# One late expert block of the first layer multiplied unsplit, in four f32 passes

## The chip, the cores and the metric

The kernel runs on one core of a Trainium2 chip. Times are device microseconds of that core. Before the change three runs gave a median of 1667.28 us (1667.20 to 1667.38). The profile is of one further execution of the same program.

## What is computed

The program is a two-layer transformer block over 256 latent tokens and 256 context tokens of width 1024, all in float32. Each layer mixes the tokens (layer 0 by a Fourier part and grouped-query attention, layer 1 by neighbourhood attention), normalises, and then sends every token through 8 of 64 small experts and through one shared expert. In layer 0 there are 512 tokens, so 4096 pairs of token and expert. The part that the change touches is the expert:

```python
def expert_block(args):
    tok, e = args
    xb = h_pad[tok]
    a = jax.nn.silu(xb @ w_gate[e]) * (xb @ w_up[e])   # 1024 -> 256, twice
    return a @ w_down[e]                                # 256 -> 1024
```

The results are weighted by the routing scores and summed per token, then layer 0 ends with a normalisation and layer 1 begins.

## The kernel before

**Jobs.** The experts of a layer are ranked by how many tokens they have, and packed by a fixed plan (class `Plan`) into jobs of 128 slots, in four lanes of 32. Layer 0 has 42 jobs (0 to 41). A job with two experts runs them beside one another in separate strips of TensorE; a job with one segment uses the full array (jobs 6, 11, 15, 20, 25, 29, 34 and 39 in layer 0). Job 39, the third from the end, is the last one with a single expert.

**The steps of a job j** stand in the loop in `moe` (L1780 and on). TensorE and SyncE follow the order in which the program is written there; VectorE, ScalarE and GpSimd are ordered by the planner. TensorE does: gate and up products of job j (16 products of 128x128 with 256 columns when it is a full-array job); the transposes of the token rows of job j+1 in two halves (`slots_T`, L1459); between them four pieces of the scatter of an earlier job and the transposes of the activations (`act_T`, L1308); the down products (4 of 512 columns); and then the rest of the earlier job's scatter (L1544). A scatter piece is two products with a selection matrix, whose sum VectorE adds to `acc` (L1536).

**Two ways to multiply.** A list `passes` holds 3 or 4 for each job. With 4 (`gate_up` L1337, `down` L1351) the float32 operands go to TensorE as they are, and the trace has two matmul records for each product. With 3 (`gate_up3`, `down3`) weights and activations are split into a high and a low float32r part: a cast on ScalarE and a subtraction on VectorE (`split`, L161), and then three products (`mm3`, L165 to L167), one record each. Gate and up take four splits of 128x1024, down takes two, `xT` (by `slots_T`) and `aT` (by `act_T`) are split as well. The parts of the weights live in the pool `k4` of 13 buffers and, for one of the six, in `t8` of four.

**Weights.** They come from memory on SyncE's queue, 1 MB at a time, into the ring `w8` of 11 buffers; `experts` issues those of a job, in the order gate, up, down, when buffers are free. A job with two experts takes six buffers, one with a single expert three. A buffer is free when its last reader is through: TensorE's products for 4 passes, the splits for 3. Behind the loads of job 41 stand, in the same queue, four reloads of the residual rows (`xr`, L1791) and the first weights of layer 1 (`preload_na`, L848 and L855).

**Other work beside the last jobs.** For some jobs the results were added to a table in memory instead (`send`). Those sums come back in four fetches of 1 MB (`fetch`, L1525) at jobs 35 to 38, and VectorE adds them one job later (`add_fetched`, L1533), so two additions of 128x1024 at each of jobs 36 to 39. After job 41 comes the normalisation of layer 0, a loop for overfull experts (`overflow_blocks`, L1642) at whose head all engines meet, and layer 1.

Of the kernel before, what the change touches and what calls it, by code (L numbers as in the profile page):

```python
# [118 lines left out]
def tile_block(ctx: ExitStack, tc: tile.TileContext, I, out):  # L119
# [940 lines left out]
    def moe(l, out_of, nt, mp, pre=lambda: None, post=lambda: None):  # L1060
# [156 lines left out]
        njob = len(jobs)  # L1217
# [457 lines left out]

        passes = []
        for sg_ in jobs:
            passes.append(3 if l == 0 and len(sg_) == 1 and len(passes) > 2 else 4)
        grp, sc = [], iter(())
        over = overflow()  # L1680
        LA = 3 if l == 0 else 2
# [253 lines left out]
    with tc.tile_pool(name="moe0", bufs=1) as mp:  # L1935
        normalize(moe(0, out0, 4, mp, preload_na, mods_na)[0], xt[:2])
# [3 lines left out]
    with tc.tile_pool(name="moe1", bufs=1) as mp:  # L1940
        y = moe(1, out1, 2, mp)[1]
        for t in range(2):
            for n in range(1 + t):
                r = slice(n * 512, n * 512 + D // (1 + t))
                S.dma_start(out[0, t * 128:t * 128 + 128, r], y[t][:, r])
# [85 lines left out]
```

## Time and profile before

| what | value |
| --- | --- |
| median of three runs | 1667.28 us |
| profiled execution | 1667.79 us |
| its span, first to last instruction | 1666.0 us |
| TensorE (PE) busy | 1560.8 us, 94% |
| VectorE (DVE) busy | 762.9 us, 46% |
| ScalarE (ACT) busy | 444.3 us, 27% |
| GpSimd (POOL) busy | 174.0 us, 10% |
| mean granted TensorE clock | 0.980 |
| memory traffic | 332 GB/s over the span |

Busy shares are means over stages that differ. TensorE is pipelined, so what counts for it is when one group starts after another, and where the trace shows it idle and what ended that. A timeline row gives the start in us, how long the group lasted, the engine, the line, what was written from what, how many instructions were merged into the row, and in brackets the idle time ahead of it with what ended it. PEld, the load of the stationary operand, runs beside PE. SPq is SyncE's queue of transfers. In a row of stretches, the number behind an engine is its busy time, PEclk is the granted TensorE clock as a share of full speed (1.00 is 2.4 GHz, 0.50 is 1.2 GHz), and DMA is the mean busy share of the 16 DMA engines.

### The profile page before, as it was taken

The page shows a single profiled execution, that of the slowest core. Times are in us where ns is not written, and L with a number is a line of the kernel's source. Part 1 is how long each engine was busy: PE and PEld are TensorE (multiplying, and loading weights), DVE is VectorE, ACT ScalarE, POOL GpSimd, SP SyncE. Part 2 cuts the span into 40 slices and gives each one's busy share as a digit, 9 for nine tenths or more (in the row PEclk, how much of TensorE's full clock was granted, in tenths as well). Part 3 has the DMA queues.
Part 4 walks back from the last instruction along what each step waited for, and adds up shares of the span by engine and source line. Part 5 has one row for each costly group of instructions (what it writes and reads, how often), then busy time and mean ns, then how long its engine had stood idle before and what let it go on. Part 6 is the DMA issues. An engine that isn't in the chain of part 4 may idle for free. (4 is left out here: it accounts for less than half of the span.)

```text
span 1666.0 us, 30733 instructions
## 1 busy us (share of the span) xinstructions
PE 1560.8 (94%) x12138; PEld 1005.9 (60%) x12138; DVE 762.9 (46%) x2077; ACT 444.3 (27%) x882; POOL 174.0 (10%) x162
## 2 busy tenths in 40 slices
PE   7999999999999999999998799999999988989995
PEld 5765687546556566565665577866756654546542
DVE  2475585425455445354566832347443422223225
ACT  2447311113132232232222243332222211112111
POOL 1003210123221121221110000011000000000000
PEclk9999999999999999999999899999999999999998
DMA  9947864799999999989998566247779999999994
GB/s 331 340 172 290 297 233 162 268 366 382 346 398 345 402 401 389 392 327 406 404 407 309 205 212 222 89 181 309 303 316 420 419 419 419 419 420 419 419 420 179
DMA packets 122819, 547.91 MB, mean 329 GB/s; under 512 B 12917, under 2 KB 21509, under 8 KB 74672
## 3 DMA queue, kind: packets, MB, share of 16 engines
q1 hardware_dynamic: 108032, 501.76, 75.6%
q0 software_dynamic: 14640, 44.15, 8.6%
q8 instruction: 97, 1.59, 0.4%
q14 instruction: 50, 0.41, 0.1%
HBM read 532.10 MB, written 21.58 MB: 332 GB/s over the span
## 5 line engine op out<-in xcount | busy, mean ns | idle before, releaser
L1337 PE MATMUL bank<-w,xT 128*32 128x256 f32 (+1 forms) x5696 | 462.8, 388 | 25.8 <-DMA w<-in_moe_w_up_dram 20.2
L1337 PEld LDWEIGHTS bank<-w,xT 128*32 128x32 f32 (+1 forms) x5696 | 276.5, 122 | 204.9 <-DMA w<-in_moe_w_up_dram 28.2
L1351 PE MATMUL bank<-w,aT 128*32 128x512 f32 (+2 forms) x1248 | 235.3, 599 | 3.0 <-ACT aT L1312 2.9
L1293 DVE SCALAR_TENSOR_TENSOR a<-s,wsl,bank 128x256 f32<-128x256 f32 x70 | 33.6, 480 | 407.4 <-ACT s L1292 407.4
L1292 ACT ACTIVATE s<-bank 128x256 f32<-128x256 f32 x70 | 26.9, 385 | 544.5 <-PE bank L1337 496.7
L1544 PE MATMUL bank<-yy,ss 128*128 128x512 f32 x560 | 159.0, 411 | 1.4 <-DVE yy L161 1.1
L1536 DVE TENSOR_TENSOR acc<-acc,bank 128x512 f32<-128x512 f32 x212 | 138.0, 683 | 43.3 <-PE bank L1544 41.6
L1351 PEld LDWEIGHTS bank<-w,aT 128*32 128x32 f32 (+2 forms) x1248 | 68.5, 123 | 120.0 <-issue 104.0
L1544 PEld LDWEIGHTS bank<-yy,ss 128*128 128x128 f32 x560 | 97.3, 191 | 25.9 <-DVE yy L161 5.0
L161 DVE TENSOR_TENSOR yy<-bank,yy 128x512 fp32r<-128x512 f32 x96 | 65.9, 689 | 91.7 <-ACT yy L161 91.7
L161 ACT CAST yy<-bank 128x512 fp32r<-128x512 f32 x96 | 56.2, 586 | 161.6 <-PE bank L1351 144.2
L1445 POOL DMA_INDIRECT xg<-h2d,idx x42 | 52.1, 1239 | 356.8 <-PE bank L1459 181.7
L161 DVE TENSOR_TENSOR wl<-half,wh 128x1024 fp32r<-128x1024 f32 x35 | 42.7, 1224 | 74.4 <-ACT wh L161 74.4
L1250 DVE TENSOR_SCALAR oh<-ib,pos 128x64 bf16<-128x64 bf16 (+3 forms) x432 | 68.7, 245 | 9.7 <-PE bank L1276 9.7
L1516 POOL DMA_INDIRECT accd<-yd,idx x37 | 59.4, 1605 | 128.0 <-issue 92.7
L165 PE MATMUL bank<-wh,hT 128*128 128x512 f32 x160 | 65.2, 407 | 1.7 <-ACT wh L161 1.1
L167 PE MATMUL bank<-wl,hT 128*128 128x512 f32 x160 | 63.4, 396 | 0.5 <-DVE wl L161 0.5
L166 PE MATMUL bank<-wh,hT 128*128 128x512 f32 x160 | 63.2, 395 | 0.3 <-DVE hT L161 0.2
L1485 PE MATMUL bank<-ohr,h2p 128*128 128x256 f32 x448 | 60.8, 289 | 0.0
L1485 PEld LDWEIGHTS bank<-ohr,h2p 128*128 128x128 f32 x448 | 55.3, 191 | 8.2 <-PE bank L1337 4.4
L1437 POOL TENSOR_TENSOR xr<-xr,tmp 128x512 f32<-128x512 f32 x2 | 3.3, 1649 | 478.2 <-DVE tmp L1436 478.2
L1459 PE MATMUL bank<-head,xg 128*128 128x128 f32 x336 | 52.1, 278 | 0.0
(362 smaller groups left out, 2313.2 us busy)
## 6 DMA issues: line engine op xcount, KB each, us to landing
w<-in_moe_w_gate_dram SPq DMA_DIRECT2D x128, 1024.0 KB
w<-in_moe_w_up_dram SPq DMA_DIRECT2D x128, 1024.0 KB
w<-in_moe_w_down_dram SPq DMA_DIRECT2D x104, 1024.0 KB
w<-in_w_mod_dram SPq DMA_DIRECT2D x24, 1024.0 KB
half<-in_na_w_in_dram SPq DMA_DIRECT2D x12, 1024.0 KB
mh<-in_w_mod_dram SPq DMA_DIRECT2D x12, 1024.0 KB
w<-in_w_mod_dram SPq DMA_DIRECT2D x16, 512.0 KB
row<-rowsd POOLq DMA_DIRECT2D x15, 512.0 KB, 8.3
```

The lines of the kernel that those rows point to most:

```text
L161: return A.copy(o_h, src), eng.tensor_sub(o_l, src, o_h.bitcast(F32))
L165: T.matmul(p, xh, wh, start=first, stop=False)
L166: T.matmul(p, xl, wh, start=False, stop=False)
L167: T.matmul(p, xh, wl, start=False, stop=last)
L1250: V.tensor_scalar(oh[:, 32 * lane:32 * (lane + m)], ib[:, off:off + 32 * m], pos[:, t, c:c + 1], None, op0=OP.is_equal)
L1337: T.matmul(p[sl, q * FF:q * FF + FF], xT(j, sl), ws[k][0][q][:, j], start=j == 0, stop=j == NJ - 1, **kw)
L1351: T.matmul(p[sl], aT[:, j, sl], d[:, n * 512:n * 512 + 512], start=j == 0, stop=j == 1, **kw)
L1445: G.indirect_dma_start(out=x, out_offset=None, in_=h2d[:n2, :], in_offset=bass.IndirectOffsetOnAxis(ap=idx_col, axis=0), bounds_check=n2 - ...
L1485: T.matmul(o, h2p[t][k][:, 2 * q + j], oh[:, t].rearrange("p a b -> p (a b)")[:, :n], start=t == 0 and k == 0, stop=t == nt - 1 and k == 1)
L1516: G.indirect_dma_start(out=accd[turn_[0]][:, :], out_offset=bass.IndirectOffsetOnAxis(ap=i_, axis=0), in_=y[32 * lane:32 * (lane + m)], in ...
L1536: add = {0: lambda t, r, p: V.tensor_add(acc[t][:, r], acc[t][:, r], p)}
L1544: T.matmul(p, ss[:, t * 128:t * 128 + 128], yy[:, q, r], start=k == 0 and q == 0, stop=k == len(grp) - 1 and q == 1)
```

## The change

The list `passes` gets 4 instead of 3 for a job with one segment when it is among the last three of the plan. In layer 0 this concerns job 39 alone; the other seven full-array jobs from 6 to 34 stay as they were, and layer 1 has 4 everywhere already. Job 39 then goes through `gate_up`, `down`, and the unsplit forms of `slots_T` (called at job 38) and `act_T`. The calls on SyncE's queue keep their order.

```diff
         passes = []
         for sg_ in jobs:
-            passes.append(3 if l == 0 and len(sg_) == 1 and len(passes) > 2 else 4)
+            passes.append(3 if l == 0 and len(sg_) == 1 and 2 < len(passes) < njob - 3 else 4)
```

The functions that job 39 leaves:

```python
def gate_up3(x, w):
    p = bank()
    for k in range(4):
        wh, wl = gu_parts(w, k)          # cast on ScalarE, subtraction on VectorE
        ...
        for j in range(4):
            ...
            mm3(o, x[0](J, ...), x[1](J, ...), wh[:, j], wl[:, j], J == 0, J == NJ - 1)
    return p

def down3(aT, w):
    ps = [bank(), bank()]
    for j in range(2):
        wh, wl = w_parts([128, D], w[1][:, j, :], V)
        for n in range(2):
            ...
            mm3(ps[n], aT[0][:, j, :], aT[1][:, j, :], wh[:, r], wl[:, r], j == 0, j == 1)
    return ps
```

## Rows read from the trace of the kernel before

**Rows 1.** First line of the page: span and instructions.
```profile
span 1666.0 us, 30733 instructions
```
**Rows 2.** Timeline of PE, job 38: gate and up, transposes, down, rest of the scatter.
```profile
847.23 7.13 PE L1337 MATMUL bank<-w,xT 128*64 128x256 f32 x64
854.28 0.66 PE L1459 MATMUL bank<-head,xg 128*128 128x128 f32 x4
...
857.39 3.65 PE L1351 MATMUL bank<-w,aT 128*64 128x512 f32 x16
860.97 2.11 PE L1544 MATMUL bank<-yy,ss 128*128 128x512 f32 x8
```
**Rows 3.** Timeline of PE, job 39 and the start of job 40.
```profile
862.92 0.28 PE L165 MATMUL bank<-wh,xT 128*128 128x256 f32 x1
...
866.37 0.58 PE L167 MATMUL bank<-wl,xT 128*128 128x256 f32 x1 [3.06 <-DVE wl L161]
...
869.53 0.28 PE L166 MATMUL bank<-wh,xT 128*128 128x256 f32 x1
...
873.36 0.60 PE L1459 MATMUL bank<-head,xg 128*128 128x128 f32 x4
...
876.33 0.39 PE L165 MATMUL bank<-wh,aTh 128*128 128x512 f32 x1
878.31 0.49 PE L166 MATMUL bank<-wh,aTl 128*128 128x512 f32 x1 [1.60 <-DVE aTl L161]
880.64 0.80 PE L167 MATMUL bank<-wl,aTh 128*128 128x512 f32 x1 [1.83 <-DVE wl L161]
881.24 0.63 PE L165 MATMUL bank<-wh,aTh 128*128 128x512 f32 x1
...
885.08 2.71 PE L1544 MATMUL bank<-yy,ss 128*128 128x512 f32 x8
887.72 7.13 PE L1337 MATMUL bank<-w,xT 128*64 128x256 f32 x64
```
**Rows 4.** Timeline of DVE at job 39: additions, then splits of the gate weights.
```profile
862.71 2.47 DVE L1536 TENSOR_TENSOR acc<-acc,bank 128x512 f32<-128x512 f32 x4
865.09 2.36 DVE L161 TENSOR_TENSOR wl<-w,wh 128x1024 fp32r<-128x1024 f32 x2
```
**Rows 5.** Busy times in stretches: after the first stall, job 38, job 39.
```profile
866.40:869.40 3.00, 3.00 (x14) 3.00 (x15) 2.83 (x3) 0.00 (x0) 0.00 (x0) 0.50 1.02 419
...
847.20:862.90 15.70, 15.70 (x107) 9.68 (x107) 9.96 (x17) 5.25 (x9) 2.13 (x3) 1.00 1.02 421
862.90:887.70 24.80, 18.31 (x87) 15.31 (x85) 16.88 (x22) 6.43 (x10) 1.05 (x2) 0.79 0.87 344
```
**Rows 6.** Timeline of PE in layer 1: a full-array job in four passes.
```profile
1272.67 7.17 PE L1337 MATMUL bank<-w,xT 128*128 128x256 f32 x32
1279.50 2.26 PE L1485 MATMUL bank<-ohr,h2p 128*128 128x256 f32 x16
...
1283.68 3.59 PE L1351 MATMUL bank<-w,aT 128*128 128x512 f32 x8
1287.11 0.25 PE L1276 MATMUL bank<-wt,oh 128*128 128x15 bf16 x4
```
**Rows 7.** Timeline of SyncE's queue: up and down weights of job 41.
```profile
867.48 2.87 SPq L1069 DMA_DIRECT2D w<-in_moe_w_up_dram  x2
881.75 9.99 SPq L1074 DMA_DIRECT2D w<-in_moe_w_down_dram  x2
```
**Rows 8.** Busy times in stretches of 5 us: two with little traffic.
```profile
885.00:890.00 5.00, 5.00 (x31) 3.42 (x31) 3.42 (x6) 0.59 (x1) 0.00 (x0) 0.84 0.18 72
...
920.00:925.00 5.00, 4.12 (x15) 1.73 (x12) 3.05 (x5) 0.83 (x2) 0.00 (x0) 0.93 0.00 0
```
**Rows 9.** Timeline of POOL: the last fetch; then the landing of tile `ad`.
```profile
858.33 1.10 POOL L1525 DMA_DIRECT2D ad<-accd  x2 [0.48 <-issue]
...
DMA to landing us min/median/max: 14.8/14.8/14.8
```

## The prediction

> **What bounds the kernel now.** I read the page first, then TensorE's timeline around job 39, then VectorE's over the same time, then the transfers. The span is 1666.0 us [rows 1]; the profiled execution took 1667.79 us, so 1.79 us lie outside the span, and it stands 0.51 us above the median of 1667.28. TensorE is busy in 94% of it, so a change counts if it lets TensorE's queue reach a later point sooner and nothing else has to be waited for there.
>
> Job 38 shows how a job runs undisturbed: it starts at 847.23 and the next at 862.92 (first row of rows 3), 15.69 us, with TensorE busy throughout at a clock of 1.00 and VectorE busy for 9.96 us [rows 2, 3, 5]. Job 39 starts at 862.92 and job 40 at 887.72: 24.80 us, mean clock 0.79 [rows 3, 5]. The reader should see three bracketed waits in it, all for VectorE: 3.06 us for the first low part of the gate weights, 1.60 for the low part of the activations, 1.83 for a low part of the down weights, together 6.49 us [rows 3]. VectorE is not idle then. At 862.71 it still has four additions of 2.47 us in all, and only at 865.09 does it begin the subtractions that TensorE wants [rows 4]. So in this stage VectorE sets the pace, and TensorE's clock falls behind each wait: 0.50 from 866.4 to 869.4 [rows 5], and the 512-column products at 881.24 last 0.63 us [rows 3].
>
> **The change, part by part.** (1) Gate and up. In layer 1 a full-array job does them unsplit: its 32 records start at 1272.67 and the next group at 1279.50, so 6.83 us [rows 6]. Job 39 took from 862.92 to 873.36, 10.44 us [rows 3]. Saved: 3.61 us.
>
> (2) Down. The same job in layer 1 takes 1283.68 to 1287.11, 3.43 us [rows 6]. Job 39 took 876.33 to 885.08, 8.75 us [rows 3]. Saved: 5.32 us.
>
> (3) The rest of the scatter behind it: 2.64 us in job 39 (885.08 to 887.72), 1.95 us in job 38 (860.97 to 862.92), the same eight products [rows 2, 3]. The former start at the lower clock that the waits left. Saved: 0.69 us, if no wait is left in the job. The piece between gate and down is 2.97 us in job 39 (873.36 to 876.33) and 3.11 in job 38 (854.28 to 857.39). I take job 38's, so 0.14 is lost.
>
> Sum: 3.61 + 5.32 + 0.69 - 0.14 = 9.48 us. As a check, 15.69 of job 38 less 0.22 (gate and up 7.05, from 847.23 to 854.28, to 6.83) and 0.15 (down 3.58, from 857.39 to 860.97, to 3.43) is 15.32, and 24.80 - 15.32 = 9.48.
>
> In other words the products themselves get dearer: 48 records at 0.120 us (869.53 to 873.36, 32 of them) are 5.75 us against 6.83, and 12 at about 0.214 (half of the 0.427 us at which they follow one another from 881.24 to 885.08 at the low clock) are 2.56 against 3.43. That is 1.95 us lost. It is repaid by 6.49 us of waits and by the clock, which makes up the rest.
>
> Here a rule can be weighed. The trace has a split product at 0.120 us for 256 columns and pass, an unsplit one at 6.83 / 16 = 0.427 us, a ratio of 1.19 to the 0.359 of three parts [rows 3, 6]. The Trainium skill, "FP8 and Floating Point Precision", section "TensorE Precision Notes", says that true FP32 takes four passes through the array. Taken as a price of four passes to the split's three it would make 5.75 into 7.67 us and 2.56 into 3.41, and the sum 8.7 instead of 9.48; the row of layer 1 has the very operation, so I go by that.
>
> (4) ScalarE and VectorE lose the splits: six of 128x1024, at 2.36 / 2 = 1.2 us each on VectorE [rows 4], two of `xT` and one of `aT`. TensorE then waits for none of them. What remains on it are the two copies of `xT` and one of `aT` by ScalarE, which job 38 does as well while TensorE is busy for all of its 15.70 us [rows 5]. VectorE has some 10 us of work in a job of 15.3.
>
> (5) What is late next. The last fetch is issued at 858.33 in two parts, 0.55 us apart, and landing takes 14.8 us [rows 9]: 873.1 and 873.7. Before, VectorE reached these additions late. Now the activations of job 39 are through at about 862.92 + 6.83 + 0.7 = 870.5, and VectorE may stand for up to 2.6 us before the first addition. Behind it on VectorE are the scatter's additions, which free accumulator banks. TensorE needs such a bank only at the second half of the scatter, behind down, at about 876.3, when at least one has been freed. Bounds: 0 and 2.6 us; I take 0.2, near the lower end, since job 38 has the same two additions with TensorE busy throughout [rows 5].
>
> (6) Transfers. The order on SyncE's queue stays. The up weights of job 41 wait for job 39's gate and up buffers: 867.48 and some 2.5 us later before; now gate is read out at 862.92 + 3.4 = 866.3 and up at 869.8, no later. Its first down weight waited for the splits until 881.75 [rows 7]; now it is free at 876.3, its second when job 40 has used a gate, 878.2 + 3.5 = 881.7 instead of 891.4. The engines idle at 885 to 890 (0.18) shows that the queue had nothing left over by then [rows 8], so the weights of job 40 and the up weights of job 41 had landed by about 883. Job 40's, issued before those, are needed from 878.2, job 41's up from 897.6 + 3.5. Cost: 0; without this cover job 40 would wait for at most the 885 - 878 = 7 us until the traffic falls.
>
> (7) Behind it. At 920 to 925 no transfer runs at all [rows 8]: layer 1's first weights are there before layer 0's end wants them, and all of layer 1 is issued behind the meeting of the engines at the loop. So a shift of layer 0's end moves layer 1 as a whole, its stretch bound by transfers too. What can differ is where the clock falls: the down products of job 41 and the first products of layer 1 run partly at the lower clock. The nearest size is the 3.00 us at 0.50 behind job 39's first wait, which costs 1.5 us [rows 5]: one such more or less, -1.5 to +1.5; I take 0.
>
> Forecast: -9.48 + 0.2 = -9.28 us. Span 1666.0 - 9.3 = 1656.7, execution 1667.79 - 9.3 = 1658.5, and 0.51 lower for the median: **1658.0 us**.
>
> **The rivals.** A: VectorE is late anyway. Then the same 6.49 us of waits stay, in front of the scatter or of job 40, and the clock falls behind them as before; what is left is the dearer product, so 1667.28 + 1.95 = 1669.2 at worst, and 1667.28 - 9.48 + 6.49 = 1664.3 if the clock holds. For it: VectorE carries the fetched additions in these jobs. Against it: job 38 has them too, and 9.96 of 15.70 us [rows 5]. 5%.
>
> B: The gain is given back in front of layer 1, because its first weights or the residual rows come when they came before: 1667.3. For it: the DMA engines are at 1.02 through job 38 [rows 5]. Against it: they fall to 0.18 and later to 0.00 [rows 8], and what they wait for moves forward with the jobs. 4%.
>
> C, on the other side: the clock. Unsplit products at full array might be granted 1.2 GHz, as in the stretch at 0.50 [rows 5]. If the whole of job 39 ran so, it would take 2 x 15.32 = 30.6 us, 5.8 more than now: 1673.1. It turns slower when more than 9.5 of the 15.3 us are lost, so when over 62% of the job runs at the low clock. For it: this is where the clock falls now. Against it: each fall has a wait of TensorE ahead of it, job 38 in unsplit products stands at 1.00, and layer 1's full-array job runs at 0.2135 us a record, 512 columns at 2.4 GHz [rows 5, 6]. 4%. The Trainium skill, "TensorE: Matmul & The Clock Gate", Part 1, holds that idleness brings the throttle and activity releases it; by that rule C falls away, and the rows of job 38 and 39 agree.
>
> That the change touches nothing can be excluded: job 39 has one segment and stands at 42 - 3.
>
> **How the numbers follow.** The forecast has 87%. Its own bounds are the 2.6 us for the fetch in place of 0.2 and 1.5 us of clock either way: -9.48 - 1.5 = -11.0 gives 1656.3, -9.48 + 2.6 + 1.5 = -5.4 gives 1661.9. For the order that the planner gives VectorE and ScalarE, which this profile can't show, I add some tenths below. The range is 1655.5 to 1662.0; the rivals lie outside it with 13%. A measurement of this kernel can tell about 0.2%, 3.3 us, from no change. Faster by more than that: the forecast and a small part of A, 0.88. Within: most of A, and B, 0.08. Slower: C, 0.04.
>
> **What would show it.** Job 39 should start at about 863 and job 40 15.3 us later, with 32 records of gate and up over 6.8 us and 8 of down over 3.4, no wait for VectorE above 0.5 us between them, and a clock of 1.00. The zero traffic ahead of the loop and everything in layer 1 should come 9 to 9.5 us sooner. A wait of VectorE for the fetched sums of about 2.5 us may appear. The prediction is wrong if job 40 starts later than 881, if TensorE waits for a bank or a weight there, or if job 39 is short and layer 1 doesn't move with it.

## The result, and the profile after

The change took the median from 1667.28 us to 1657.09 (five runs, 1656.43 to 1660.99), a ratio of 0.994 with an interval of 0.9928 to 0.9952. The forecast was 1658.0. In a second measurement on another occasion it was 1657.65 against 1667.16, again 0.994 (0.9927 to 0.9954). The profiled execution took 1656.43 us, 1654.3 of them the span, 11.7 less than the span of before [rows 1].

TensorE's timeline of the changed kernel, job 39 from 862.50 and the start of job 40 (columns as in [rows 3]):

```profile
862.50 7.07 PE L1337 MATMUL bank<-w,xT 128*128 128x256 f32 x32
869.40 0.60 PE L1459 MATMUL bank<-head,xg 128*128 128x128 f32 x4
...
872.35 3.59 PE L1351 MATMUL bank<-w,aT 128*128 128x512 f32 x8
875.38 2.40 PE L1544 MATMUL bank<-yy,ss 128*128 128x512 f32 x8
877.71 7.13 PE L1337 MATMUL bank<-w,xT 128*64 128x256 f32 x64
```

No row has a bracketed wait, nor has any of the rows left out. The job takes 15.21 us (862.50 to 877.71) where it took 24.80 [rows 3]. VectorE in the same stretch:

```profile
870.48 1.22 DVE L1533 TENSOR_TENSOR acc<-acc,ad 128x1024 f32<-128x1024 f32 x1
871.61 0.68 DVE L1536 TENSOR_TENSOR acc<-acc,bank 128x512 f32<-128x512 f32 x1
873.29 1.23 DVE L1533 TENSOR_TENSOR acc<-acc,ad 128x1024 f32<-128x1024 f32 x1 [1.00 <-DMA ad<-accd]
```

It now stands for 1.00 us for the second fetched sum, and TensorE's rows above have no wait for it. Busy times in job 39, and at the place where layer 0 ends (PE, PEld, DVE, ACT, POOL, PEclk, DMA, GB/s):

```profile
862.50:877.70 15.20, 15.20 (x67) 11.44 (x65) 8.51 (x14) 3.10 (x6) 0.00 (x0) 1.00 1.02 414
...
910.00:915.00 5.00, 4.12 (x17) 2.73 (x16) 4.05 (x7) 0.59 (x1) 0.00 (x0) 1.00 0.00 0
```

The clock is at 1.00 throughout the job, against a mean of 0.79 [rows 5], and transfers run dry before layer 0 ends, as in [rows 8]. The timeline of SyncE's queue for the same loads as in [rows 7]:

```profile
866.14 3.79 SPq L1069 DMA_DIRECT2D w<-in_moe_w_up_dram  x2
875.98 5.77 SPq L1074 DMA_DIRECT2D w<-in_moe_w_down_dram  x2
```

The down weights go out 5.8 us sooner, at once when job 39's down products have read theirs. TensorE's timeline at the job of layer 1 that [rows 6] show:

```profile
1260.80 7.17 PE L1337 MATMUL bank<-w,xT 128*128 128x256 f32 x32
```

It started at 1272.67 and now starts at 1260.80, 11.87 us sooner, about as much as the whole span is shorter. So nothing was given back in layer 1. Job 39 itself accounts for 9.59 us of the 11.87. It began 0.42 sooner already, by chance (job 0 was 1.8 us sooner in this execution, ahead of everything that the change touches), and the down products of job 41 ran at the full clock this time, 3.65 us in the timeline of after:

```profile
906.60 3.65 PE L1351 MATMUL bank<-w,aT 128*64 128x512 f32 x16 [0.75 <-ACT aT L1312]
```

The same products in the timeline of before took 5.35 us:

```profile
916.59 5.35 PE L1351 MATMUL bank<-w,aT 128*64 128x512 f32 x16 [0.76 <-ACT aT L1312]
```

Together they are 11.7 us. The first experiment shows that the 1.7 us are not the change's.

### The profile page after: what moved, and what is told of

The parts are those of the page before. It is cut to its first block, busy times and chain, and to the rows that moved or that the text cites. A ratio compares the mean times of both kernels' runs of the same rounds, so it can differ in the third digit from the quotient of the medians.

```text
span 1654.3 us, 30681 instructions
## 1 busy us (share of the span) xinstructions
PE 1557.6 (94%) x12118; PEld 1002.7 (61%) x12118; DVE 754.4 (46%) x2068; ACT 438.1 (26%) x876; POOL 173.6 (10%) x162
## 5 line engine op out<-in xcount | busy, mean ns | idle before, releaser
L1337 PE MATMUL bank<-w,xT 128*32 128x256 f32 (+2 forms) x5728 | 473.0, 391 | 23.0 <-DMA w<-in_moe_w_up_dram 18.6
L1337 PEld LDWEIGHTS bank<-w,xT 128*32 128x32 f32 (+2 forms) x5728 | 285.3, 124 | 203.3 <-issue 30.3
L1292 ACT ACTIVATE s<-bank 128x256 f32<-128x256 f32 x70 | 26.9, 384 | 543.7 <-PE bank L1337 491.9
```

The costliest lines, as they stand in the source:

```text
L1337: T.matmul(p[sl, q * FF:q * FF + FF], xT(j, sl), ws[k][0][q][:, j], start=j == 0, stop=j == NJ - 1, **kw)
```

## The experiments

All ratios are against runs of the kernel before on the same chip; the medians of those lay between 1667.16 and 1668.83 us.

### The change again

No edit.

> The changed kernel once more, as the yardstick for the runs beside it. Theory (VectorE's lateness and the clock behind it were the price of the split): about 1657, and job 39 takes 15.2 us with the clock at 1.00. What differs between executions should be where the clock falls behind job 39: in the profile of the change the down products of job 41 took 3.65 us, in that of the kernel before 5.35; if this is chance and not the change, some executions of either kernel have it.

Measured: 1657.65 us, 0.994 (0.9927 to 0.9954). Job 39 from 865.24 to 880.46 is 15.22 us. TensorE's timeline at the start of jobs 39 and 40 and at job 41:

```profile
865.24 7.07 PE L1337 MATMUL bank<-w,xT 128*128 128x256 f32 x32
...
880.46 7.13 PE L1337 MATMUL bank<-w,xT 128*64 128x256 f32 x64
...
908.09 0.50 PE L1308 MATMUL bank<-head,a 128*128 128x128 f32 x2 [1.09 <-DVE a L1293]
909.35 5.33 PE L1351 MATMUL bank<-w,aT 128*64 128x512 f32 x16 [0.75 <-ACT aT L1312]
```

The same program has 5.33 us here and had 3.65 in the execution shown above, behind the same two waits of 1.09 and 0.75 us. The mean clock is 0.76 from 908 to 915 here and was 1.00 from 905.3 to 912.3 there. So where the clock falls behind job 39 differs from execution to execution. Of the twelve profiles in this document five have 5.3 us at this place (the one of before among them) and seven 3.65, all behind the same two waits. This execution also reached job 39 2.7 us later than the first. Its span is 1658.5 us, 4.2 more than the first. The runs of the changed kernel spread by about 5 us, so single executions can't be compared to better than that; the length of job 39 within them can.

### Each half alone

Gate and up unsplit, down split (the changed kernel with three passes in the down half of job 39):

```diff
+        pdown = [3 if l == 0 and j == njob - 3 else q for j, q in enumerate(passes)]
...
-                aT = act_T(a, passes[j])
+                aT = act_T(a, pdown[j])
...
-                ps = down3(aT, ws[0]) if passes[j] == 3 else down(aT, ws, segs)
+                ps = down3(aT, ws[0]) if pdown[j] == 3 else down(aT, ws, segs)
```

> Job 39 multiplies gate and up unsplit in four passes, down still split in three. Theory: about 3.5 us less than before from gate and up (10.44 to 6.9 us); VectorE, rid of four subtractions, is then in time for the down parts as well, so most of the 1.60 and 1.83 us of waits and the low clock go too: 1659 to 1661. Rival (each half pays for itself alone): 1667.3 - 3.6 = 1663.7, and the down half still takes 8.7 us.

Measured: 1664.62 us, 0.9987 (0.9975 to 0.9999), 0.9 us above the rival's number and 3.6 above the upper end of the theory's. TensorE's timeline, job 39 and the start of job 40:

```profile
861.30 7.07 PE L1337 MATMUL bank<-w,xT 128*128 128x256 f32 x32
868.21 0.60 PE L1459 MATMUL bank<-head,xg 128*128 128x128 f32 x4
...
874.43 0.50 PE L166 MATMUL bank<-wh,aTl 128*128 128x512 f32 x1 [2.87 <-DVE aTl L161]
876.76 0.80 PE L167 MATMUL bank<-wl,aTh 128*128 128x512 f32 x1 [1.82 <-DVE wl L161]
881.19 2.49 PE L1544 MATMUL bank<-yy,ss 128*128 128x512 f32 x8
883.62 7.13 PE L1337 MATMUL bank<-w,xT 128*64 128x256 f32 x64
```

Gate and up take 6.91 us as forecast, but the job is 22.32 us long, only 2.48 shorter than before. The first wait of down grew from 1.60 us [rows 3] to 2.87, so the down half takes 10.02 us (871.17 to 881.19) where the rival had it at 8.7. VectorE shows why:

```profile
869.28 1.22 DVE L1533 TENSOR_TENSOR acc<-acc,ad 128x1024 f32<-128x1024 f32 x1
870.41 0.68 DVE L1536 TENSOR_TENSOR acc<-acc,bank 128x512 f32<-128x512 f32 x1
872.22 1.23 DVE L1533 TENSOR_TENSOR acc<-acc,ad 128x1024 f32<-128x1024 f32 x1 [1.13 <-DMA ad<-accd]
873.36 0.68 DVE L1536 TENSOR_TENSOR acc<-acc,bank 128x512 f32<-128x512 f32 x1
873.96 0.42 DVE L161 TENSOR_TENSOR aTl<-bank,aTh 128x256 fp32r<-128x256 f32 x1
```

The low part of the activations stands behind two fetched additions, and the second of these waits for its transfer. TensorE came sooner and met a queue that could not come sooner. My theory for this run had taken VectorE's queue as work alone and left the transfer out.

Gate and up split, down unsplit (the kernel before, with the same three lines but `pdown = [4 if l == 0 and j == njob - 3 else q ...]`):

> Job 39 multiplies gate and up split in three passes, down unsplit in four. Theory: the wait of 3 us in gate stays, with the low clock behind it; down goes from 8.75 to 3.4 us and the scatter behind it to 1.95: 1667.3 - 6 = 1661.3, between 1660.5 and 1662.5. Rival (the waits move on to the scatter and to job 40 because VectorE stays late): 1664 or more.

Measured: 1661.13 us, 0.9966 (0.9953 to 0.9979): 6.0 us less than before, as the theory had it. TensorE's timeline:

```profile
862.31 0.28 PE L165 MATMUL bank<-wh,xT 128*128 128x256 f32 x1
...
865.71 0.58 PE L167 MATMUL bank<-wl,xT 128*128 128x256 f32 x1 [3.00 <-DVE wl L161]
...
875.72 3.60 PE L1351 MATMUL bank<-w,aT 128*128 128x512 f32 x8
878.75 2.40 PE L1544 MATMUL bank<-yy,ss 128*128 128x512 f32 x8
881.08 7.13 PE L1337 MATMUL bank<-w,xT 128*64 128x256 f32 x64
```

In these rows of TensorE's timeline the wait in gate is there, 3.00 us, and the down half has none. The two halves alone are worth 2.48 us and (862.31 to 881.08) 24.80 - 18.77 = 6.03; together 8.5, while the whole change shortens the job by 9.59. The rest, 1.1 us, is what the gate half loses again: 1.27 us in the down split's longer wait, less 0.21 that it gains in the scatter behind it (2.43 us for 2.64).

### Why VectorE was late

The kernel before, job 39 split, without the fetched additions of jobs 38 and 39. Two of the four token tiles lack the sums that were sent to memory.

```diff
+                if l == 0 and j in (njob - 4, njob - 3):
+                    added.clear()
                 add_fetched()
```

> The kernel before, three passes in job 39, but the sums that were fetched for two of the four token tiles are not added at jobs 38 and 39 (four additions of 1.22 us on VectorE are left out). Theory (VectorE is late at job 39 because of its queue, and the split alone is not dear): the first wait falls from 3.06 to about 0.6 us, those of down from 3.43 to under 1.8, the clock holds in part: 1658 to 1661, nearly the gain of the change with the split kept. Rival (the split of the job is too slow by itself, casts and parts come one by one): waits of over 5 us stay, 1665 or more.

Measured: 1658.97 us, 0.995 (0.9936 to 0.9965). TensorE's waits in job 39, with its first row and that of job 40:

```profile
863.34 0.28 PE L165 MATMUL bank<-wh,xT 128*128 128x256 f32 x1
...
866.42 0.39 PE L167 MATMUL bank<-wl,xT 128*128 128x256 f32 x1 [1.25 <-DVE wl L161]
...
874.51 0.50 PE L166 MATMUL bank<-wh,aTl 128*128 128x512 f32 x1 [0.54 <-DVE aTl L161]
876.84 0.50 PE L167 MATMUL bank<-wl,aTh 128*128 128x512 f32 x1 [0.44 <-DVE wl L161]
...
879.78 7.13 PE L1337 MATMUL bank<-w,xT 128*64 128x256 f32 x64
```

Four additions of 1.22 us, 4.9 us of VectorE, are gone, and with the split kept TensorE's job shrinks by 24.80 - 16.44 = 8.36 us (863.34 to 879.78). The waits fall from 6.49 to 2.23 us, 4.26 (the first is 1.25 us where 0.6 was expected). The other 4.1 are the clock: the same products keep TensorE busy for 14.27 us where it was 18.31 [rows 5], and the busy times of its job 39 show

```profile
863.30:879.80 16.50, 14.27 (x89) 11.86 (x88) 12.71 (x19) 5.52 (x9) 1.06 (x2) 1.00 1.01 415
```

a clock of 1.00, where it was 0.79 [rows 5]. It did not fall behind the wait of 1.25 us here; in job 39 of before it was low behind the wait of 3.06 us, and behind that of 1.83 with one of 1.60 shortly ahead of it [rows 3].

More changed than the length of VectorE's work. Without the additions the planner also sets VectorE's instructions in another order, and in VectorE's timeline the first subtraction for job 39's gate weights stands in job 38,

```profile
859.46 1.22 DVE L161 TENSOR_TENSOR wl<-w,wh 128x1024 fp32r<-128x1024 f32 x1
```

ahead of the scatter's last additions, where it was at 865.09 behind them [rows 4]. So the run shows that VectorE's queue made the split dear, and not how much of the 8.36 us is the additions' own and how much the new order's.

The changed kernel, job 39 unsplit, with the six weight splits still made for nobody:

```diff
+                if l == 0 and j == njob - 3:
+                    for k in range(4):
+                        gu_parts(ws[0], k)
                 p = pre_p.pop(j, None) or (gate_up3(xT, ws[0]) if passes[j] == 3 else gate_up(xT, ws, segs))
...
+                if l == 0 and j == njob - 3:
+                    for k in range(2):
+                        w_parts([128, D], ws[0][1][:, k, :], V)
                 ps = down3(aT, ws[0]) if passes[j] == 3 else down(aT, ws, segs)
```

> The changed kernel, job 39 unsplit, but the six weight splits (cast on ScalarE, subtraction on VectorE, 128x1024 each) are still made at job 39 and their parts are read by nothing. Theory (what cost was that TensorE waited for parts at the end of VectorE's queue, not the work itself): TensorE meets no part, only accumulator banks that VectorE frees later; job 39 takes 15.3 to 17.5 us and the whole 1657 to 1660. Rival (VectorE's and ScalarE's work itself holds the jobs up, through banks, through buffers of k4 or through the weight buffers that the splits keep): job 39 takes 20 us or more, 1662 to 1667.

Measured: 1658.18 us, 0.9952 (0.9939 to 0.9966). TensorE's timeline at the start of jobs 39 and 40, and the busy times of job 39:

```profile
863.78 7.07 PE L1337 MATMUL bank<-w,xT 128*128 128x256 f32 x32
...
879.00 7.13 PE L1337 MATMUL bank<-w,xT 128*64 128x256 f32 x64
...
863.80:879.00 15.20, 15.20 (x67) 11.44 (x65) 12.23 (x16) 5.44 (x9) 1.06 (x2) 1.00 1.01 415
```

VectorE does 12.23 us of work instead of the 8.51 of the changed kernel, and the job takes 15.22 us all the same (863.78 to 879.00). That is 3.7 us more and not the 7.2 of six splits, since the first ran in job 38 (from 861.01) and the last two, from 877.34 to 879.69, pushed other work into job 40. Job 40 takes 19.42 us, as in the changed kernel, so nothing is paid there either. The weight splits as work cost TensorE nothing; what cost was that it stood for their results. The splits of `xT` and `aT` are not in this run.

Gate and up unsplit, down split, and the fetches one job earlier:

```diff
-                if sent and j - max(sent) in range(2, 2 + nt):
-                    fetch(j - max(sent) - 2)
+                if sent and j - max(sent) in range(1, 1 + nt):
+                    fetch(j - max(sent) - 1)
```

> As in the run with gate and up unsplit and down split, and the four fetches of sums are issued one job earlier (jobs 34 to 37 instead of 35 to 38), so that VectorE has no such additions at job 39. Theory (in the run before, the wait for the activation's low part grew from 1.60 to 2.87 us because the second fetched addition stood 1.13 us for its transfer and two additions of 1.22 us lay ahead): the waits of down fall from 4.69 us to about 1.0, as in job 34, job 39 takes about 16 us, the whole 1657 to 1659. Rival (the down split is late whatever VectorE has ahead of it): waits above 3 us stay, 1663 or more.

Measured: 1658.25 us, 0.9954 (0.994 to 0.9967), 6.4 us less than the same kernel with the fetches where they were. TensorE's timeline at the start of job 39, at down, and at the start of job 40:

```profile
862.96 7.07 PE L1337 MATMUL bank<-w,xT 128*128 128x256 f32 x32
...
873.78 0.50 PE L166 MATMUL bank<-wh,aTl 128*128 128x512 f32 x1 [0.56 <-DVE aTl L161]
876.11 0.50 PE L167 MATMUL bank<-wl,aTh 128*128 128x512 f32 x1 [0.42 <-DVE wl L161]
...
879.07 7.13 PE L1337 MATMUL bank<-w,xT 128*64 128x256 f32 x64
```

The waits of down fall from 4.69 us to 0.98 and the job, 862.96 to 879.07, to 16.11. Nothing is left out here, so the finding of the run without the fetched additions doesn't hang on the missing sums. The edit takes the additions and the wait for their transfer out of job 39 together; what each of the two cost was not tried.

### The other full-array jobs

All eight unsplit (`passes.append(4)`):

> All eight full-array jobs of layer 0 multiply unsplit. By the rows, a job that is not disturbed takes about 5.8 + 4.5 us split (0.9 us of it waits for the parts of activation and down weights) and 6.83 + 3.43 us unsplit, the same; the seven jobs have 13 us of waits in all, of which some 4 are beyond that. Theory (the split is worth nothing where VectorE is busy, and nothing is lost by leaving it): 1653 to 1658, same as the change or a little less. Rival (three passes are the cheaper way where VectorE is in time, by 1.95 us a job): 1657 + 7 x 1.95 = 1671.

Measured: 1649.75 us, 0.9904 (0.989 to 0.9919), and in a second measurement, for which this stood,

> All eight full-array jobs of layer 0 unsplit, once more, beside the mixed version on the same chip: 1649 to 1651, and 8 us under the change by jobs 6 to 34.

1649.84 us, 0.9894 (0.9877 to 0.991). That is 7.3 us under the change's median, which was measured on another occasion, and below the 1653 to 1658 of the first expectation. In the profiles the time from the silu of job 5 to that of job 35 is 417.33 and 417.35 us with all unsplit, and 425.76 and 424.24 in the two of the changed kernel, so 6.9 to 8.4 us less. Down unsplit in all eight, gate and up split in the other seven:

```diff
+        pdown = [4] * njob
...
-                aT = act_T(a, passes[j])
+                aT = act_T(a, pdown[j])
...
-                ps = down3(aT, ws[0]) if passes[j] == 3 else down(aT, ws, segs)
+                ps = down3(aT, ws[0]) if pdown[j] == 3 else down(aT, ws, segs)
```

> The changed kernel, and the other seven full-array jobs keep gate and up split in three passes but multiply down unsplit in four. By the rows down is 4.5 us split, waits of 0.9 included, and 3.43 unsplit, so about 1.1 us a job. Theory (TensorE's queue sets the pace in layer 0): 7 x 1.1 = 7.7 us less than the change, about 1650. Rival (the transfers, at a busy share of 0.98 from 340 to 800 us, set it): about 1657, and waits for weights appear.

Measured: 1652.87 us, 0.9921 (0.9907 to 0.9934), 4.2 us under the change's median instead of 7.7. To see where, I took the time from one silu (ScalarE, L1292) to the next but one, which holds gate and up of the job and its down:

| job | 6 | 11 | 15 | 20 | 25 | 29 | 34 | 39 |
| --- | --- | --- | --- | --- | --- | --- | --- | --- |
| before | 27.78 | 27.30 | 31.16 | 27.10 | 27.08 | 29.66 | 26.91 | 40.43 |
| change | 27.78 | 28.84 | 29.66 | 27.10 | 27.09 | 31.13 | 26.91 | 30.91 |
| all unsplit | 26.98 | 26.27 | 27.95 | 27.45 | 27.23 | 27.24 | 27.24 | 30.91 |
| down unsplit, gate split | 27.00 | 26.53 | 28.86 | 26.29 | 27.41 | 30.26 | 26.10 | 30.92 |

Where a split job runs undisturbed, with no wait in gate and up (20, 25, 34), unsplit is 0.15 to 0.35 us dearer. Where it isn't (15 and 29) unsplit is 1.7 to 3.9 us cheaper. My expectation had taken jobs 6, 11, 15 and 29 for less disturbed than they are. In the timeline of the changed kernel TensorE begins job 29 like this:

```profile
714.57 0.39 PE L165 MATMUL bank<-wh,xT 128*128 128x256 f32 x1 [1.66 <-ACT wh L161]
715.83 0.39 PE L167 MATMUL bank<-wl,xT 128*128 128x256 f32 x1 [0.76 <-DVE wl L161]
```

and the run with only down unsplit keeps such waits, 30.26 us (and has one of 0.74 us at job 25). With all eight unsplit no wait for parts is left.

The first two lines of the table differ by up to 1.5 us at jobs 11, 15 and 29, where both kernels do the same. That is the clock again. In the kernel before, TensorE waits 1.66 and 0.76 us at job 29 just as above; the busy times around it, first before and then after, show

```profile
716.00:724.00 8.00, 6.81 (x54) 6.56 (x55) 4.87 (x6) 3.66 (x6) 0.00 (x0) 1.00 1.01 426
714.00:722.00 8.00, 6.67 (x41) 6.47 (x42) 4.93 (x5) 3.36 (x4) 0.00 (x0) 0.79 1.02 428
```

a clock of 1.00 in the one execution and 0.79 in the other. The two profiles of the kernel with all unsplit agree to 0.01 us at all eight jobs.

Split gate and up only where they paid, in jobs 20 and 34, everything else unsplit (the last kernel with `passes.append(3 if l == 0 and len(passes) in (20, 34) else 4)`):

> Each full-array job of layer 0 in the form that its own rows favour: down unsplit in all eight, gate and up unsplit in six, split at jobs 20 and 34 only, where the step took 26.29 and 26.10 us with the split gate against 27.45 and 27.24 without it. Theory (TensorE's queue sets the pace, so the steps' savings add up): 2.3 us under the run with all eight unsplit. Rival (what one job saves the next waits for, or the transfers at a busy share of 0.99 take it): the same as that run within 1 us.

Measured: 1645.88 us, 0.9872 (0.9855 to 0.9889), beside 1649.84 for all unsplit on the same chip. From the silu of job 5 to that of job 35 it takes 415.04 us against 417.33, 2.29 less, and the two steps are 26.27 and 26.10 us, so the savings added up as expected. Of the rest of the 4 us, 1.5 in the two profiles lie ahead of job 5, where both kernels do the same. This is the fastest version tried, 11 us under the change's median, which was measured on another occasion.

## Why the prediction was right

**Gate and up, down.** Forecast savings were 3.61 and 5.32 us. Gate and up now take 6.90 us (862.50 to 869.40) for 10.44, down 3.03 (872.35 to the next group at 875.38) for 8.75. By the records the scatter behind down starts 0.4 us earlier than I had it and lasts 2.33 us, to 877.71; the two together are 5.36 us, and the steps gave 5.38. The sum was 9.48, measured was 9.59, and three other profiles of unsplit jobs 39 agree (15.22, 15.22, and 30.91 over the two steps with all unsplit). The layer 1 job was the right row to price by, and with the count of passes in the Trainium skill ("FP8 and Floating Point Precision", "TensorE Precision Notes") as a price the sum of 8.7 would have been 0.9 too low.

**The split's own price.** I put the products at 1.95 us dearer unsplit, which treats the split form as free of waits. In the traces of before and after every split job has waits for its parts. Even in job 34 of the changed kernel, with VectorE in time, TensorE's timeline has waits in down:

```profile
796.02 0.50 PE L166 MATMUL bank<-wh,aTl 128*128 128x512 f32 x1 [0.56 <-DVE aTl L161]
796.36 0.40 PE L167 MATMUL bank<-wl,aTh 128*128 128x512 f32 x1
...
797.52 0.40 PE L166 MATMUL bank<-wh,aTl 128*128 128x512 f32 x1
798.35 0.50 PE L167 MATMUL bank<-wl,aTh 128*128 128x512 f32 x1 [0.43 <-DVE wl L161]
```

The table shows an undisturbed split job only 0.15 to 0.35 us cheaper. The split products of down were mis-sized as well. I had halved the 0.427 us of the low clock to 0.214; at the full clock the six from 796.36 to 797.52 follow one another at 0.232, so twelve are 2.8 us and not 2.56, and the 1.95 should have been 1.7. That step mis-sized the alternative, not the forecast, which took both lengths from rows.

**VectorE late, and the clock behind it.** The runs show this: leaving out 4.9 us of additions with the split kept, in an order that the planner changed with it, gave 8.36 us; splits that nobody waits for cost nothing; and fetching one job earlier took 3.7 us of waits out of the split down half. The prediction's words that the clock falls behind each wait go too far. In job 39 of before it did so at two of the three: behind that of 1.60 us it was still 1.00, from 878.3 to 878.8. Whether it falls also differs between executions, as jobs 29 and 41 show.

**What is late next.** The wait for the fetch came, 1.00 us and only at the second addition, since the first sum had landed by 870.48. I had given both parts the one landing time that the trace of before shows, 14.8 us. It varies: GpSimd's timeline of after has the issue of the two parts, and below it stands the landing of tile `ad` in the run with gate and up unsplit and down split:

```profile
857.91 1.10 POOL L1525 DMA_DIRECT2D ad<-accd  x2 [0.48 <-issue]
...
DMA to landing us min/median/max: 8.9/11.7/14.9
```

So the first part took at most 12.6 us. My 2.6 us was an upper bound, the 0.2 that I took was more than was due, and TensorE paid none of it. Its importance I had underrated in another place: with down split it goes straight to TensorE, as the gate half alone showed.

**Transfers and layer 1.** As forecast: down weights at 875.98 for 876.3, traffic dry before the loop, layer 1 moved as a whole, by the 9.59 us of job 39 and the 2.1 us that come and go. Rival A fell with the missing waits, B with 1260.80 in layer 1, C with a clock of 1.00 through 15.2 us of full-array four-pass products. On the Trainium skill's rule ("TensorE: Matmul & The Clock Gate", Part 1) that activity releases the throttle, the trace agrees as far as it goes: job 39, busy throughout, stays at 1.00.

**The size.** 1657.09 against 1658.0 forecast is 0.9 us, less than the executions differ among themselves. The profile's 11.7 us has the clock's 1.7 us at job 41 in it. I had named such a fall with 1.5 us as a bound and not counted it, rightly, since it comes and goes.

## What to carry to other kernels

A form that saves TensorE passes by giving another engine work is worth only what that engine's queue allows at that place: compare whole jobs in the trace, waits and the clock behind them included, where the engine is free and where it isn't, and choose for each place. A split can be cheap as work and dear as a dependence. When a step is taken off the path, look at what the next instruction of the late engine waits for, here a transfer, which landed 7.6 to 15.4 us after its issue in the profiles of these runs, before adding the halves of a change.

## What the runs showed of the hardware that was not expected

Waits of TensorE cost more than their length. In job 39 6.49 us of waits came with a mean clock of 0.79, and taking 4.26 us of waits away gave 8.36. Whether short waits bring the clock down varies between executions of one program: behind the same 1.09 and 0.75 us at job 41 the same 16 products took 3.65 us in one and 5.33 in another. At job 29 the same waits of 1.66 and 0.76 us came with a mean clock of 1.00 in the profile of before and 0.79 in that of the changed kernel, and the step was 1.5 us longer. What decides it was not tried.
